# The normalised memory of a cross-attention trunk moved from SBUF to DRAM, with nine weight buffers in place of eight

## The chip, the cores and the metric

The kernel runs on one core of a Trainium2 chip. The metric is the device time of one execution in microseconds (us). The kernel before takes 1259.96 us, the median of three runs (1259.71 to 1259.99). One further execution was profiled; every trace reading below comes from that one.

## The reference

A trunk of two layers works on 256 tokens of width 1024 in float32. Each layer is half a SwiGLU feed-forward, a token mixer, a cross-attention into 256 memory tokens, and another half feed-forward. The mixer is a differential attention in layer 0 and a Mamba-2 SSD in layer 1.

```python
for i in range(DEPTH):                        # 2 layers
    h = h + 0.5 * swiglu(rmsnorm(h, ffn1_norm[i]), ffn1_w_gate[i], ffn1_w_up[i], ffn1_w_down[i])
    hn = rmsnorm(h, mix_norm[i])
    h = h + (diff_attention if i == 0 else ssd_mixer)(hn, ...)
    h = h + memory_cross_attention(rmsnorm(h, xa_norm[i]), mem, xa_mem_norm[i], xa_w_q[i], xa_w_kv[i], xa_w_o[i])
    h = h + 0.5 * swiglu(rmsnorm(h, ffn2_norm[i]), ffn2_w_gate[i], ffn2_w_up[i], ffn2_w_down[i])
return rmsnorm(h, final_norm)
```

The part that the change handles is the memory. `memory_cross_attention` computes `m = rmsnorm(mem, mem_norm)` and from it keys and values, `m @ w_kv`. The RMS factor of `mem` is the same in both layers; only the gain `xa_mem_norm[i]` differs.

## The kernel before, in words

**Weights.** All weights are streamed from HBM once, in tiles `w` of 128 partitions x 2048 float32 (1 MB, 8 KB of each partition). Their pool `wp` has eight buffers. `W.load` (L161) and `Pair.load` (L176) issue the loads on SyncE (SP); a load waits on SP until the buffer that it takes was read for the last time, and the loads behind it on SP wait with it. Every weight is used in two parts, so that float32 accuracy comes out of the fast float32r matmul: a "granule" of 1024 columns is cast on ScalarE (ACT) to `whi` (L224), and VectorE (DVE) forms the rest `wlo` (L225). Both have four buffers, and granules are cut two ahead of their use (`AHEAD`). TensorE (PE) then runs `mm3` (L262 to L264): hi x hi, lo x hi and hi x lo.

**Feed-forward.** A hidden width of 2816 is done in columns c = 0 to 4 of 512 and a half one. The first feed-forward does c = 2, 3 and 4 with a scheme of seven products in place of eight (`seven`, tile name `seven`), the three later ones c = 1 to 4. For it, sums of weight tiles are formed before they are cut. Two of the four sums of each c are DVE additions of whole tiles (`Sum.load`, L203, 128 x 2048 elements); the two others are accumulating DMAs that GpSimd (POOL) issues (L199). DVE works in order: a sum whose tile has not landed holds up every `wlo` behind it. Between the products of `seven`, granules of the down projection and of other columns (tile names `out`, `gate`, `up`) are woven in.

**Memory.** `mem_stage` loads the memory tokens in four tiles `mnat` (L685) during the first feed-forward, and `mem_prep` (L688) scales them by their RMS factor. `turn` (L701) then transposes them, two 128 x 128 transposes on PE into a PSUM tile `tin` and one ACT copy (L705), eight times, into eight tiles `memt[j]` of 128 x 256 in the `const` pool; they stay there (8 KB of each partition) to the end. Two users read them. `MemKV.prep` multiplies them by the layer's gain and splits them, `mh` on ACT (L457) and `ml` on DVE (L459), for the key and value projections. `MemKV.mix` (L1071) multiplies them once more into four tiles `my` of the pool of 28 general buffers ("slots", 128 x 512), and `combine` makes from these the sums which `seven` needs for the value projection.

**Where these run.** Hooks in the program call them. Layer 0: `prep` after the first value columns (L1006), `mix` at step (0, 4) of the mixer's out projection (`out_b`, L1043). Layer 1: `prep` first in the first feed-forward, by the key 12 (L1607), which `extras(6)` calls in the middle of column 4; `prep` again and then `mix` in the out projection of the SSD mixer at steps (1, 4) and (0, 8) (L1519). The steps of `out_b` run in the order (0, k), (1, k) for each block k.

**Order.** Only the very start is ordered by hand on every engine, and the SSD stretch on PE. Elsewhere the framework's scheduler orders each engine's instructions, so a change in one place can move instructions elsewhere.

Of the kernel before, what the change touches and what calls it, by code (L numbers as in the profile page):

```python
# [7 lines left out]
F32 = mybir.dt.float32  # L8
F32R = mybir.dt.float32r
BF16 = mybir.dt.bfloat16  # L10
I32 = mybir.dt.int32
AF = mybir.ActivationFunctionType
# [3 lines left out]
P = 128  # L16
S = 256
D = 1024
KT = D // P
# [38 lines left out]
def trunk(ctx, tc, a, out):  # L58
    nc = tc.nc


    const = ctx.enter_context(tc.tile_pool(name="const", bufs=1))
    wp = ctx.enter_context(tc.tile_pool(name="wp", bufs=8))
    hp = ctx.enter_context(tc.tile_pool(name="hp", bufs=4))
    xp = ctx.enter_context(tc.tile_pool(name="xp", bufs=8))
    sp = ctx.enter_context(tc.tile_pool(name="sp", bufs=28))
# [3 lines left out]
    dram = ctx.enter_context(tc.tile_pool(name="dram", bufs=1, space=bass.MemoryType.DRAM))  # L70

    def slot(name, dt=F32):
        return sp.tile([P, 512], dt, name=name, tag="s")

    def acc(name):
        return pacc.tile([P, 512], F32, name=name, tag="acc")

    def small_ps(name):
        return pacc.tile([P, 512], F32, name=name, tag="acc")

    def work(name, n=512, dt=F32):

        return wk.tile([P, n], dt, name=name, tag="v", bufs=6) if n <= 256 else wk.tile([P, n], dt, name=name, tag="w")


    ident = const.tile([P, P], F32, name="ident")
# [53 lines left out]
    pipe = Pipe()  # L140
# [96 lines left out]
    def use(gr):  # L237

        for g in gr:
            ready(g.at + AHEAD + 1)  # L240
            yield g
# [19 lines left out]
    def mm3(o, lh, ll, rh, rl, start, stop, onto=False):  # L261
        nc.tensor.matmul(o, lhsT=lh, rhs=rh, start=start, stop=False, skip_group_check=onto)  # L262
        nc.tensor.matmul(o, lhsT=lh, rhs=rl, start=False, stop=False, skip_group_check=onto)  # L263
        nc.tensor.matmul(o, lhsT=ll, rhs=rh, start=False, stop=stop, skip_group_check=onto)  # L264
# [161 lines left out]
    def out_b(src, nkt, lhs, fin, order, hooks={}):  # L426


        banks = [[], []]
        first, last = order[0], order[-1] + 3  # L430

        def run(*gr, half):
            if not banks[half]:
                banks[half] += [acc("out") for _ in range(2)]
            for g in use(gr):
                for k in range(g.nk):
                    kt = g.k0 + k
                    for t in range(2):
                        xh, xl = pipe.need(lhs, kt)
                        ts = slice(t * P, (t + 1) * P)  # L440
                        mm3(banks[half][t], xh[:, ts], xl[:, ts], g.hi[:, k, :], g.lo[:, k, :], kt == first, kt == last)
                        pipe.pe(0.68)
                    if kt == last:
                        fin(half, banks[half])
        for half, k0 in [(c, k) for k in order for c in range(2)]:
            if (half, k0) in hooks:
                units.append(([], hooks[half, k0]))
            w = W(src, k0, 4, half * 512, 512)
            for k in range(k0, k0 + 4, 2):
                units.append(([Gran(k, 2, (w, 0, 512))], lambda *gr, half=half: run(*gr, half=half)))  # L450

    def split_act(dst_hi, dst_lo, src, scale):

        if not isinstance(src, (list, tuple)):
            dst_hi, dst_lo, src, scale = [dst_hi], [dst_lo], [src], [scale]
        for h_, s_, c_ in zip(dst_hi, src, scale):
            nc.scalar.activation(h_, s_, AF.Copy, scale=c_)  # L457
        for h_, l_, s_, c_ in zip(dst_hi, dst_lo, src, scale):
            nc.vector.scalar_tensor_tensor(l_, s_, c_, h_.bitcast(F32), op0=ALU.mult, op1=ALU.subtract)  # L459
# [34 lines left out]
    class Norm:  # L494
# [68 lines left out]
        def turn(self, c):  # L563
            for i in range(2):
                ps = self.flip(c, i)
                self.put(4 * c + 2 * i, ps[:, 0, :], ps[:, 1, :])
# [9 lines left out]
    def v2(t, j=2):  # L576
        return t.rearrange("p (j t) -> p j t", j=j)

    def upd(scale, norm):
        def fin(c, ps):  # L580
            for t in range(2):
                if scale == 1.0:
                    nc.vector.tensor_tensor(h[t][c], ps[t], h[t][c], op=ALU.add)
                else:
                    nc.vector.scalar_tensor_tensor(h[t][c], ps[t], scale, h[t][c], op0=ALU.mult, op1=ALU.add)
            norm.add(c)
        return fin
# [57 lines left out]
    lqk2 = lqk  # L645
    lqk = lqk.rearrange("p (k d) -> p k d", k=4)
    subln = cols0[:, KT:KT + 1]
    memt = [const.tile([P, S], F32, name=f"mem{j}") for j in range(KT)]
    mcol = const.tile([P, 16], F32, name="mcol")
    mnat = [[None, None], [None, None]]  # L650
    cols1 = const.tile([P, P], F32, name="cols1")
# [7 lines left out]
    def gains(nm, l=0):  # L659
        o = rowpos[nm] + l * KT  # L660
        return cols1[:, o:o + KT]
# [26 lines left out]
    def mem_prep():  # L688
        mss = sm.tile([P, 16], F32, name="mss", tag="mss", bufs=1)
        for t in range(2):  # L690
            for c in range(2):
                junk = work("junkm", 512)
                nc.scalar.activation(junk, mnat[t][c], AF.Square, accum_out=mss[:, 2 * c + t:2 * c + t + 1])
        nc.vector.tensor_tensor(mss[:, 4:6], mss[:, 0:2], mss[:, 2:4], op=ALU.add)
        nc.vector.tensor_scalar(mcol[:, 2:4], mss[:, 4:6], 1.0 / D, EPS, op0=ALU.mult, op1=ALU.add)
        nc.gpsimd.tensor_tensor(mcol[:, 0:2], mcol[:, 2:4], neghalf[:, 0:2], op=ALU.pow)
        for t in range(2):
            for c in range(2):
                nc.scalar.activation(mnat[t][c], mnat[t][c], AF.Copy, scale=mcol[:, t:t + 1])

        def turn(j):  # L701
            ps = small_ps("tin")
            for t in range(2):
                nc.tensor.transpose(ps[:, t * P:(t + 1) * P], mnat[t][j // 4][:, (j % 4) * P:(j % 4 + 1) * P], ident)
            nc.scalar.copy(memt[j], ps[:, :S])  # L705
        for j in range(KT):
            pipe.after(6.0 + 1.0 * j, lambda j=j: turn(j))


    def mem_stage():  # L710
# [184 lines left out]
    def diff_attention(norm, nxt, kv):  # L895
# [4 lines left out]
        ot = [None] * 8  # L900
# [42 lines left out]

        def proj_fin(key):
            def fin(ps):
                if not tab:
                    def late():
                        tables()
                        rope(ps, key)
                    pipe.after(T["gate"], late)  # L950
                    return
                rope(ps, key)
            return fin
# [86 lines left out]
        for c in range(2):  # L1040
            wide([(w_in, 2048 + c * 512, 512)], norm, "v", v_fin(2 * c))
        kv.k_units(kv.k_split, cs=(0,))
        out_b(a["da_w_out"][0], KT, ot, upd(1.0, nxt), (0, 4), {(0, 4): kv.mix})  # L1043


    def split2(src, name):
# [7 lines left out]
    class MemKV:  # L1054


        def __init__(self, l):
# [4 lines left out]
            self.x = []  # L1062
            self.s = [None] * 4

        def mix(self):
            y = [slot("my") for _ in range(KT // 2)]

            def full(p):
                for j in range(2):
                    k = 2 * p + j  # L1070
                    nc.scalar.activation(v2(y[p])[:, j, :], memt[k], AF.Copy, scale=self.g[:, k:k + 1])  # L1071
            for p in range(KT // 2):
                pipe.after(1.4 * p, lambda p=p: full(p))
            combine(y, self.s, [7.0 + 1.6 * i for i in range(8)])
# [3 lines left out]

        def prep(self):
            self.x.clear()  # L1080
            for j in range(KT):
                if j % 2 == 0:
                    mh, ml = slot("mh", F32R), slot("ml", F32R)
                xh, xl = (m[:, j % 2 * S:(j % 2 + 1) * S] for m in (mh, ml))
                split_act(xh, xl, memt[j], self.g[:, j:j + 1])
                self.x.append((xh, xl))

        def k_units(self, then=None, cs=(0, 2)):
            def fin(c):
# [105 lines left out]
    def ssd(norm, nxt, kv):  # L1195
# [13 lines left out]
        yt = [None] * 16  # L1209
# [293 lines left out]
        for i in range(4):  # L1503
# [3 lines left out]
            def xs(j):  # L1507
                proj("a", w_in, 2048 + 512 * i + 256 * j, 256, norm, "xs", [fx[j]])
# [7 lines left out]
                     lambda ps, fz=fz: [f([p[:, j * 256:(j + 1) * 256] for p in ps]) for j, f in enumerate(fz)])  # L1516
            if i < 3:
                xs(1)
        out_b(a["ssd_w_out"][0], 16, yt, upd(1.0, nxt), (0, 4, 8, 12), {(1, 4): kv.prep, (0, 8): kv.mix})  # L1519
        written.append(len(units))  # L1520


# [80 lines left out]
    kvs = [MemKV(0), MemKV(1)]  # L1603
    for l in range(2):
        nx = Norm(gains("mix_norm", l), first=l == 1)
        ffn("ffn1", l, nrm, nx,
            {1: param_cols, 8: rope_tables, 9: lam_col, 12: mem_stage} if l == 0 else {12: kvs[1].prep})  # L1607
        nx2 = Norm(gains("xa_norm", l))
        kv = kvs[l]
        (diff_attention if l == 0 else ssd)(nx, nx2, kv)  # L1610
        nx3 = Norm(gains("ffn2_norm", l), mixes=True)
        cross_attention(l, nx2, kv, nx3)
        if l == 0:
            nrm = Norm(gains("ffn1_norm", 1), mixes=True)
            ffn("ffn2", l, nx3, nrm)
# [58 lines left out]
```

## Time and profile before

| what | value |
|---|---|
| median of three runs | 1259.96 us (1259.71 to 1259.99) |
| the profiled execution: its time | 1260.52 us |
| its span (first to last instruction) | 1258.7 us |
| granted TensorE clock | 0.998 |
| PE busy | 1247.5 us (99%) |
| DVE busy | 1058.3 us (84%) |
| ACT busy | 873.9 us (69%) |
| POOL busy | 161.4 us (13%) |
| moved by DMA | 269.79 MB, mean 214 GB/s |

Engines are named PE, PEld (its weight loads), DVE, ACT, POOL and SP; a "q" behind one is its instruction queue (waits and DMA issues). "L203" is line 203 of the kernel before. A row of a timeline has its start, the time from the first instruction's start to the last one's end, and behind "x" how many like instructions it joins; a bracket tells how long the engine stood idle ahead of it and what ended that.

### The profile page before, as it was taken

To read this page: it belongs to the slowest core of one execution; us is meant where nothing else is said; L and a number is where in the kernel's file an instruction comes from. 1 tells how busy PE (TensorE), PEld (TensorE's weight loads), DVE (VectorE), ACT (ScalarE), POOL (GpSimd) and SP (SyncE) were. 2 spreads that over 40 slices of the span, in tenths; PEclk is the share of its full clock that TensorE was granted. 3 is DMA by queue.
4 is the path that set the end of the run, shared out by engine and by line. 5 is a ranking of instruction groups with operands and counts; after the bars stand their busy time and mean duration, and the time that the engine had idled before them with its cause. 6 is when DMAs were issued, how large, how long until landed. Compare 5 with 4: busy or idle time off the path is not lost.

```text
span 1258.7 us, 18177 instructions
## 1 busy us (share of the span) xinstructions
PE 1247.5 (99%) x6751; PEld 1072.1 (85%) x6751; DVE 1058.3 (84%) x1451; ACT 873.9 (69%) x1392; POOL 161.4 (13%) x139
## 2 busy tenths in 40 slices
PE   9999999999999999999999999999999999999997
PEld 7887888788998888888888889999998898888886
DVE  6997887886787899888998976798899887898886
ACT  6676765586676776767776856777776766877773
POOL 1101102101100111001111000022222200011100
PEclk9999999999999999999999999999999999999999
DMA  9898965335786598986689976665643786488971
GB/s 335 261 256 236 330 236 169 133 138 159 205 236 167 157 255 272 284 268 197 178 251 277 293 245 205 201 199 168 194 142 134 179 244 185 163 228 235 291 233 34
DMA packets 158315, 269.79 MB, mean 214 GB/s; under 512 B 6889, under 2 KB 43410, under 8 KB 158226
## 3 DMA queue, kind: packets, MB, share of 16 engines
q1 hardware_dynamic: 137744, 229.75, 53.6%
q0 software_dynamic: 19744, 38.28, 17.6%
q8 instruction: 53, 0.87, 0.3%
q10 hardware_dynamic: 738, 0.59, 0.2%
q14 instruction: 36, 0.29, 0.1%
HBM read 267.52 MB, written 1.08 MB: 213 GB/s over the span
## 4 chain that ended last, share of the span: by engine, by line
PE 96%; DVE 1%; DMA 1%; issue 1%; ACT 0%; POOLq 0%; POOL 0%; SPq 0%; DVEq 0%; ACTq 0%
PE out L262 9%; PE out L264 9%; PE out L263 9%; PE seven L263 8%; PE seven L264 8%; PE seven L262 8%; PE xs L264 2%; PE xs L262 2%; PE xs L263 2%; PE htp L851 1%; PE up L264 1%; PE up L262 1%; PE up L263 1%; PE mk L262 1%; PE xq L263 1%; PE mk L264 1%
## 5 line engine op out<-in xcount | busy, mean ns | idle before, releaser
L225 DVE TENSOR_TENSOR wlo<-w,whi 128x1024 fp32r<-128x1024 f32 (+2 forms) x532 | 640.0, 1220 | 132.7 <-ACT whi L224 126.0
L224 ACT CAST whi<-w 128x1024 fp32r<-128x1024 f32 (+2 forms) x534 | 551.6, 1040 | 249.8 <-PE out L264 91.2
L262 PE MATMUL out<-whi,hid_hi 128*128 128x512 f32 x336 | 132.7, 395 | 0.0
L264 PE MATMUL out<-whi,hid_lo 128*128 128x512 f32 x336 | 131.0, 390 | 0.0
L263 PE MATMUL out<-wlo,hid_hi 128*128 128x512 f32 x336 | 130.9, 390 | 0.0
L263 PE MATMUL seven<-wlo,s_hi 128*128 128x512 f32 x272 | 106.0, 390 | 0.6 <-DVE wlo L225 0.6
L262 PE MATMUL seven<-whi,s_hi 128*128 128x512 f32 x272 | 106.1, 390 | 0.0
L264 PE MATMUL seven<-whi,s_lo 128*128 128x512 f32 x272 | 105.9, 389 | 0.0
L203 DVE TENSOR_TENSOR w<-w 128x2048 f32<-128x2048 f32 x32 | 73.2, 2287 | 5.7 <-DMA w<-in_ffn_w_gate_dram 5.3
L264 PEld LDWEIGHTS out<-whi,hid_lo 128*128 128x128 f32 x336 | 63.1, 188 | 13.4
L263 PEld LDWEIGHTS out<-wlo,hid_hi 128*128 128x128 f32 x336 | 63.2, 188 | 12.6 <-DVE wlo L225 0.2
L262 PEld LDWEIGHTS out<-whi,hid_hi 128*128 128x128 f32 x336 | 63.1, 188 | 12.4
L263 PE MATMUL seven<-wlo,xh 128*128 128x512 f32 x180 | 70.2, 390 | 1.9 <-DVE wlo L225 1.9
L199 POOL DMA_DIRECT2D w<-in_ffn_w_up_dram x30 | 36.7, 1268 | 274.4 <-DVE wlo L225 267.7
L262 PE MATMUL seven<-whi,xh 128*128 128x512 f32 x180 | 70.5, 392 | 0.0
L264 PE MATMUL seven<-whi,xl 128*128 128x512 f32 x180 | 70.1, 390 | 0.0
L199 POOL DMA_DIRECT2D w<-in_ffn_w_gate_dram x30 | 36.9, 1467 | 257.9 <-DVE w L203 114.4
L263 PEld LDWEIGHTS seven<-wlo,s_hi 128*128 128x128 f32 x272 | 51.1, 188 | 11.4 <-DVE wlo L225 1.0
L264 PEld LDWEIGHTS seven<-whi,s_lo 128*128 128x128 f32 x272 | 51.0, 188 | 10.7
L262 PEld LDWEIGHTS seven<-whi,s_hi 128*128 128x128 f32 x272 | 51.1, 188 | 10.5
L263 PEld LDWEIGHTS seven<-wlo,xh 128*128 128x128 f32 x180 | 33.8, 188 | 9.1 <-DVE wlo L225 2.3
L264 PEld LDWEIGHTS seven<-whi,xl 128*128 128x128 f32 x180 | 33.8, 188 | 7.1
(395 smaller groups left out, 3016.5 us busy)
## 6 DMA issues: line engine op xcount, KB each, us to landing
w<-in_ffn_w_up_dram SPq DMA_DIRECT2D x40, 1024.0 KB, 9.5
w<-in_ffn_w_down_dram SPq DMA_DIRECT2D x40, 1024.0 KB, 9.8
w<-in_ffn_w_gate_dram SPq DMA_DIRECT2D x38, 1024.0 KB, 6.7
w<-in_ssd_w_in_dram SPq DMA_DIRECT2D x24, 1024.0 KB, 5.5
w<-in_xa_w_kv_dram SPq DMA_DIRECT2D x16, 1024.0 KB, 5.3
w<-in_ffn_w_gate_dram POOLq DMA_DIRECT2D x30, 512.0 KB, 9.2
w<-in_ffn_w_up_dram POOLq DMA_DIRECT2D x30, 512.0 KB, 7.7
w<-in_da_w_in_dram SPq DMA_DIRECT2D x12, 1024.0 KB, 5.2
```

What stands on the lines that cost most here:

```text
L199: nc.gpsimd.dma_start(self.t[:, k:k + 2, :], w.src[r0:r0 + 2 * P, w.c0:w.c0 + w.n] .rearrange("(k p) c -> p k c", p=P), accum_op=ALU.add)
L203: nc.vector.tensor_tensor(self.t, self.l.t, w.t, op=ALU.add)
L224: nc.scalar.copy(hv, src)
L225: self.eng.tensor_tensor(self.lo[:, :, o:o + n], src, hv.bitcast(F32), op=ALU.subtract)
L262: nc.tensor.matmul(o, lhsT=lh, rhs=rh, start=start, stop=False, skip_group_check=onto)
L263: nc.tensor.matmul(o, lhsT=lh, rhs=rl, start=False, stop=False, skip_group_check=onto)
L264: nc.tensor.matmul(o, lhsT=ll, rhs=rh, start=False, stop=stop, skip_group_check=onto)
L851: nc.tensor.transpose(tp[:, j, t * P:(t + 1) * P], us[t][:, (i + j) * P:(i + j + 1) * P], ident)
```

## The change

The transposed memory `memt` becomes one DRAM tile of 128 x 2048 (1 MB). `turn` now does four transposes into one PSUM tile, one ACT copy of 128 x 512 to a slot `mt`, and one DMA write of 256 KB issued by ACT; it runs four times rather than eight. A new `fetch` takes four slots `my` and issues four 256 KB DMA reads, on ACT too. `prep` and `mix` read these slots; `mix` scales them in place. `fetch` is called four times, 16 reads in all:

- layer 0, ahead of `prep`: at the end of the second key columns (`proj_fin`, key ("k", 1));
- layer 0, ahead of `mix`: at step (0, 0) of the out projection;
- layer 1, ahead of the first `prep`: at key 12 of the first feed-forward; `prep` moves from key 12 to key 8, which is called at the end of column 4;
- layer 1, in the SSD out projection: at step (1, 4); `prep` moves from (1, 4) to (0, 8), `mix` from (0, 8) to (1, 8).

The 8 KB of each partition that this leaves free in `const` go to `wp`, which has nine buffers.

```diff
-    wp = ctx.enter_context(tc.tile_pool(name="wp", bufs=8))
+    wp = ctx.enter_context(tc.tile_pool(name="wp", bufs=9))
...
-    memt = [const.tile([P, S], F32, name=f"mem{j}") for j in range(KT)]
+    memt = dram.tile([P, KT * S], F32, name="memt")
...
-        def turn(j):
-            ps = small_ps("tin")
-            for t in range(2):
-                nc.tensor.transpose(ps[:, t * P:(t + 1) * P], mnat[t][j // 4][:, (j % 4) * P:(j % 4 + 1) * P], ident)
-            nc.scalar.copy(memt[j], ps[:, :S])
-        for j in range(KT):
-            pipe.after(6.0 + 1.0 * j, lambda j=j: turn(j))
+        def turn(i):
+            ps = v2(small_ps("tin"))
+            for j in (2 * i, 2 * i + 1):
+                for t in range(2):
+                    nc.tensor.transpose(ps[:, j % 2, t * P:(t + 1) * P], mnat[t][j // 4][:, (j % 4) * P:(j % 4 + 1) * P],
+                                        ident)
+            mt = slot("mt")
+            nc.scalar.copy(v2(mt), ps)
+            nc.scalar.dma_start(memt[:, 512 * i:512 * i + 512], mt)
+        for i in range(KT // 2):
+            pipe.after(6.0 + 2.0 * i, lambda i=i: turn(i))
...
+                if key == ("k", 1):
+                    kv.fetch()
...
-        out_b(a["da_w_out"][0], KT, ot, upd(1.0, nxt), (0, 4), {(0, 4): kv.mix})
+        out_b(a["da_w_out"][0], KT, ot, upd(1.0, nxt), (0, 4), {(0, 0): kv.fetch, (0, 4): kv.mix})
...
+        def fetch(self):
+            self.y = [slot("my") for _ in range(KT // 2)]
+            for p in range(KT // 2):
+                nc.scalar.dma_start(self.y[p], memt[:, 512 * p:512 * p + 512])
+
         def mix(self):
-            y = [slot("my") for _ in range(KT // 2)]
+            y = self.y
...
-                    nc.scalar.activation(v2(y[p])[:, j, :], memt[k], AF.Copy, scale=self.g[:, k:k + 1])
+                    nc.scalar.activation(v2(y[p])[:, j, :], v2(y[p])[:, j, :], AF.Copy, scale=self.g[:, k:k + 1])
...
-        out_b(a["ssd_w_out"][0], 16, yt, upd(1.0, nxt), (0, 4, 8, 12), {(1, 4): kv.prep, (0, 8): kv.mix})
+        out_b(a["ssd_w_out"][0], 16, yt, upd(1.0, nxt), (0, 4, 8, 12), {(1, 4): kv.fetch, (0, 8): kv.prep, (1, 8): kv.mix})
...
-            {1: param_cols, 8: rope_tables, 9: lam_col, 12: mem_stage} if l == 0 else {12: kvs[1].prep})
+            {1: param_cols, 8: rope_tables, 9: lam_col, 12: mem_stage} if l == 0 else {12: kvs[1].fetch, 8: kvs[1].prep})
```

Two places of the new order matter for the prediction. The first is DVE in layer 1's first feed-forward, where columns 2 and 3 meet. Before, it stands there (`hid_lo` is the rest of the hidden activations, `gs` the gate, `p` a product of `seven`; L203 is the sum of two weight tiles that opens column 3):

```order
L225 TENSOR_TENSOR wlo<-w,whi 128x1024 x4
L804 SCALAR_TENSOR_TENSOR gs<-gateup,rcol,gs 128x256 x2
L225 TENSOR_TENSOR wlo<-w,whi 128x1024 x3
L855 TENSOR_TENSOR hid_lo<-htp,hid_hi 128x512
L225 TENSOR_TENSOR wlo<-w,whi 128x1024 x2
L827 TENSOR_TENSOR p_6224<-seven,p_6224 128x512
L225 TENSOR_TENSOR wlo<-w,whi 128x1024
L203 TENSOR_TENSOR w<-w 128x2048
```

The same stretch of DVE with the change (its line numbers are up to 13 higher from L701 on):

```order
L225 TENSOR_TENSOR wlo<-w,whi 128x1024 x4
L808 SCALAR_TENSOR_TENSOR gs<-gateup,rcol,gs 128x256 x2
L225 TENSOR_TENSOR wlo<-w,whi 128x1024 x2
L203 TENSOR_TENSOR w<-w 128x2048
L859 TENSOR_TENSOR hid_lo<-htp,hid_hi 128x512
L225 TENSOR_TENSOR wlo<-w,whi 128x1024 x3
L831 TENSOR_TENSOR p_6229<-seven,p_6229 128x512
L225 TENSOR_TENSOR wlo<-w,whi 128x1024 x3
```

The sum has moved six instructions ahead: four `wlo`, one `hid_lo` and one product that stood before it now stand behind it. In the first feed-forward of layer 0 the sums keep their places.

The second place is ACT in the SSD out projection, at step (1, 4). Before (`mh` is the memory's high part, made straight from `mem`; `y` and `state` are the mixer's):

```order
L224 CAST whi<-w 128x1024
L1446 COPY state<-pst 128x256
L457 ACTIVATE mh<-mem_102,cols_111 128x256
L457 ACTIVATE mh<-mem_103,cols_111 128x256
L457 ACTIVATE mh<-mem_104,cols_111 128x256
L457 ACTIVATE mh<-mem_105,cols_111 128x256
L224 CAST whi<-w 128x1024
L457 ACTIVATE mh<-mem_106,cols_111 128x256
```

ACT at the same place with the change:

```order
L1459 COPY state<-pst 128x256
L1074 DMA my<-memt 128x512 x4
L224 CAST whi<-w 128x1024
L457 ACTIVATE mh<-my,cols_104 128x256
L1482 ACTIVATE junk,yss<-y 128x256 x2
L224 CAST whi<-w 128x1024
L457 ACTIVATE mh<-my,cols_104 128x256 x3
L1486 ACTIVATE y<-y,yrc 128x256 x2
```

Four reads are issued where the first `mh` stood; one cast now stands between the last read's issue and the first `mh`, which needs the first read landed.

More of the change, by code (lines that the diff above doesn't have):

```diff
@@ L1080, in prep @@
             self.x.clear()
[L1081 to L1086, printed above, removed]
+            y = self.y
+            for p in range(KT // 2):
+                mh, ml = slot("mh", F32R), slot("ml", F32R)
+                for j in range(2):
+                    k = 2 * p + j
+                    xh, xl = v2(mh)[:, j, :], v2(ml)[:, j, :]
+                    split_act(xh, xl, v2(y[p])[:, j, :], self.g[:, k:k + 1])
+                    self.x.append((xh, xl))
         def k_units(self, then=None, cs=(0, 2)):
```

## The prediction

> **What bounds the kernel now.** The page first: how busy PE is, and what the chain that ended last is made of.
>
> ```profile
> PE 1247.5 (99%) x6751; PEld 1072.1 (85%) x6751; DVE 1058.3 (84%) x1451; ACT 873.9 (69%) x1392; POOL 161.4 (13%) x139
> PE 96%; DVE 1%; DMA 1%; issue 1%; ACT 0%; POOLq 0%; POOL 0%; SPq 0%; DVEq 0%; ACTq 0%
> ```
>
> PE is busy 1247.5 of 1258.7 us, and the change leaves every matmul as it is. So at most 11.2 us are in play, and most of those lie at the ends of the program. The windows tell which do not: of all stretches of 25 us past the start only these two, besides one of 0.23 us at 775 to 800, have PE under 25.00 (columns: window, length, then busy time of PE, PEld, DVE, ACT, POOL, then granted clock, DMA share, GB/s).
>
> ```profile
> 50.00:75.00 25.00, 24.39 (x108) 19.89 (x107) 21.11 (x19) 18.96 (x23) 4.47 (x4) 1.00 1.00 261
> 100.00:125.00 25.00, 23.10 (x102) 18.61 (x101) 17.57 (x16) 14.81 (x16) 2.45 (x2) 1.00 0.87 243
> 775.00:800.00 25.00, 24.77 (x205) 24.36 (x204) 14.58 (x33) 15.99 (x29) 0.00 (x0) 1.00 0.73 230
> ```
>
> PE idles 0.61 + 1.90 + 0.23 = 2.7 us in the body of the program. The PE waits name the first two, and the PE timeline their places.
>
> ```profile
> PE seven L263 <- DVE wlo L225: 2.5, 2, 1.9
> ...
> 57.02 0.39 PE L264 MATMUL gate<-whi,xl 128*128 128x512 f32 x1
> 57.25 0.39 PE L262 MATMUL seven<-whi,s_hi 128*128 128x512 f32 x1
> 58.24 0.50 PE L263 MATMUL seven<-wlo,s_hi 128*128 128x512 f32 x1 [0.61 <-DVE wlo L225]
> ...
> 117.07 0.39 PE L262 MATMUL seven<-whi,xh 128*128 128x512 f32 x1
> 119.36 0.50 PE L263 MATMUL seven<-wlo,xh 128*128 128x512 f32 x1 [1.90 <-DVE wlo L225]
> 119.70 0.40 PE L264 MATMUL seven<-whi,xl 128*128 128x512 f32 x1
> ```
>
> Matmuls start 0.23 us apart where nothing waits (57.02 to 57.25). Start to start, the wait at 117 (call it A) costs 119.36 - 117.07 - 0.23 = 2.06 us, and its first matmul after another 0.34 - 0.23 = 0.11: 2.17 us. The wait at 57 (B) costs 58.24 - 57.25 - 0.23 = 0.76, with the same refill some 0.87 us. These two are the whole prize; both say "DVE", so the question is what held DVE.
>
> For A, DVE's timeline and the one DMA step of the chain:
>
> ```profile
> 110.58 1.21 DVE L225 TENSOR_TENSOR wlo<-w,whi 128x1024 fp32r<-128x1024 f32 x1
> 115.87 2.29 DVE L203 TENSOR_TENSOR w<-w 128x2048 f32<-128x2048 f32 x1 [4.08 <-DMA w<-in_ffn_w_gate_dram]
> 118.08 2.35 DVE L225 TENSOR_TENSOR wlo<-w,whi 128x1024 fp32r<-128x1024 f32 x2
> ...
> 106.49 9.26 DMA w<-in_ffn_w_gate_dram
> ```
>
> DVE is free at 111.79 and stands 4.08 us until the gate tile has landed at 115.75, 9.26 us after its issue. The sum, then one `wlo`, then PE: 119.36 - 115.87 = 3.49 us from sum to PE. For B:
>
> ```profile
> 49.99 3.60 DVE L225 TENSOR_TENSOR wlo<-w,whi 128x1024 fp32r<-128x1024 f32 x3 [0.57 <-ACT whi L224]
> 53.51 2.28 DVE L203 TENSOR_TENSOR w<-w 128x2048 f32<-128x2048 f32 x1
> 56.96 1.23 DVE L225 TENSOR_TENSOR wlo<-w,whi 128x1024 fp32r<-128x1024 f32 x1 [1.17 <-ACT whi L224]
> ```
>
> No load is in it: DVE works without a gap from 49.99 to 55.79, the cast waits for the sum, the `wlo` for the cast.
>
> **The change part by part.** *The ninth buffer.* A load is issued when the last reader of its buffer is done; with one buffer more, each is issued at the release that admitted its predecessor. SP's issues before A:
>
> ```profile
> 83.81 0.37 SPq L161 DMA_DIRECT2D w<-in_ffn_w_up_dram  x1
> 95.01 0.37 SPq L161 DMA_DIRECT2D w<-in_ffn_w_down_dram  x1
> ...
> 104.65 0.37 SPq L161 DMA_DIRECT2D w<-in_ffn_w_down_dram  x1
> 106.49 5.70 SPq L161 DMA_DIRECT2D w<-in_ffn_w_gate_dram  x2
> ```
>
> The gate load of A thus moves from 106.49 to 104.65, the down load of 95.01 to 83.81. What the queues do meanwhile:
>
> ```profile
> 92.00:96.00 4.00, 4.00 (x20) 3.29 (x19) 4.00 (x6) 2.75 (x5) 0.00 (x0) 1.00 0.00 1
> 96.00:100.00 4.00, 4.00 (x19) 3.34 (x18) 2.99 (x4) 2.10 (x3) 2.46 (x2) 1.00 0.97 277
> 108.00:116.00 8.00, 8.00 (x37) 6.63 (x36) 3.79 (x5) 6.19 (x7) 0.00 (x0) 1.00 1.05 389
> ```
>
> They move nothing from 92 to 96 and are full from 96 to 116. The down tile of 1 MB goes into that hole, which takes 1 MB / 389 GB/s = 2.7 us off the backlog. The gate load then lands between 104.65 + 9.26 = 113.9 (the same flight time) and 115.75 - 1.84 - 2.7 = 111.2 (issue and backlog both earlier); I take the middle, 112.5. For A to vanish, the sum must start by 115.87 - 2.06 = 113.8, so the load must land by 113.7. Gain 2.17 us, with 0 to 0.3 left over; I take 0.1. Lost altogether (0) if the backlog, not the issue, sets the landing and nothing moves.
>
> B stays: the order of DVE there is the old one, and no load waits. The 0.2 us at 775 to 800 is of another kind and stays.
>
> *Fewer, longer turns.* PE goes to the memory's transposes four times rather than eight. Each excursion has its toll in the matmul behind it:
>
> ```profile
> 180.53 0.48 PE L262 MATMUL out<-whi,hid_hi 128*128 128x512 f32 x1
> 180.84 0.39 PE L263 MATMUL out<-wlo,hid_hi 128*128 128x512 f32 x1
> 181.08 0.40 PE L264 MATMUL out<-whi,hid_lo 128*128 128x512 f32 x1
> ```
>
> 0.31 us instead of 0.23, so 0.08 each; four fewer make -0.3 us. It is on the path, since PE is busy there. The transposes themselves stay sixteen.
>
> *ACT's DMAs.* 4 writes and 16 reads are issued on ACT, which issues nothing of the kind in the body now. Price, from the two pairs at the end:
>
> ```profile
> 1251.38 0.86 ACTq L1570 DMA_DIRECT2D out_dram<-h  x2
> ```
>
> 0.43 us each, 8.6 us of ACT in all, at most 1.7 us in one go. ACT is 69% busy, and casts run two granules ahead (5.4 us of PE for two granules of 12 matmuls), so a burst of 1.7 us hides: 0. Its worst place is the SSD out projection, where the first `mh` stands one cast behind the reads and holds every later cast until its tile has landed:
>
> ```profile
> 961.50 1.71 ACT L457 ACTIVATE mh<-mem,cols 128x256 fp32r<-128x256 f32 x4
> 965.53 1.06 ACT L224 CAST whi<-w 128x1024 fp32r<-128x1024 f32 x1 [2.33 <-PE out L264]
> ```
>
> The cast after it had 2.33 us to spare even so. Against that stands a landing for which no such 256 KB read exists before; its ends are its bytes alone (0.26 MB / 389 GB/s = 0.7 us) and A's 9.26 us. At 5 us, ACT would wait 1 to 2 us within the slack; 0, up to +2 at the far end. The other three fetches stand five granules or more ahead of their use: 0. I put +0.2 here for all.
>
> A fetch carries 1 MB, 2.7 us of the queues. Two places bound whom it meets:
>
> ```profile
> 700.00:706.00 6.00, 6.00 (x31) 5.01 (x31) 5.88 (x6) 4.14 (x6) 0.00 (x0) 1.00 1.05 388
> 935.00:985.00 50.00, 50.00 (x252) 42.01 (x251) 46.12 (x72) 34.47 (x70) 14.38 (x11) 1.00 0.49 150
> ```
>
> In the SSD projection half of the queues' time is free. In layer 1's feed-forward (about 705) they are full, so a weight load there lands up to 2.7 us later. [...] I price it at 0, since the same loads start a step earlier.
>
> *Moved sums.* In the three later feed-forwards the scheduler, seeing a buffer more, puts the opening sum (L203) of columns 2, 3 and 4 ten, six and three instructions ahead. Column 3 of layer 1's first one is the tightest:
>
> ```profile
> 638.99 0.37 SPq L161 DMA_DIRECT2D w<-in_ffn_w_down_dram  x1
> 646.01 0.37 SPq L161 DMA_DIRECT2D w<-in_ffn_w_gate_dram  x1
> ...
> 643.63 2.36 DVE L225 TENSOR_TENSOR wlo<-w,whi 128x1024 fp32r<-128x1024 f32 x2 [0.45 <-ACT whi L224]
> 646.47 1.22 DVE L225 TENSOR_TENSOR wlo<-w,whi 128x1024 fp32r<-128x1024 f32 x1 [0.48 <-ACT whi L224]
> ...
> 650.64 0.39 PE L262 MATMUL out<-whi,hid_hi 128*128 128x512 f32 x1
> ...
> w<-in_ffn_w_gate_dram SPq DMA_DIRECT2D x38, 1024.0 KB, 6.7
> ```
>
> The sum now starts when the `wlo` pair ends, 645.99, or when its tile has landed. Behind it stand a `hid_lo` (0.6) and the `wlo` of 646.47, which PE needs at 650.64 + 0.23 = 650.87. Sum 2.2 + 0.6 + 1.2 = 4.0, so the sum must start by 646.8. Its load is now issued at about 639.0 to 639.4; with the median flight of 6.7 us it lands at 645.7 to 646.1: just in time. With A's flight of 9.26 it lands at 648.3 to 648.7, and PE stalls 1.5 to 1.9 us. I take the median, with +0.2 for all nine sums (0 to 5).
>
> **Sum:** -2.17 + 0.1 - 0.3 + 0.2 + 0.2 = -2.0 us; I give it as -1.9, the ACT place being the least known. The profiled execution goes from 1260.52 to 1258.6; it lies 0.56 above the median, so the median goes from 1259.96 to 1258.1. A measurement of this kernel tells about 0.2% (2.5 us) from no change, so this is "the same": faster by that would need under 1257.4.
>
> **The rivals.**
>
> *1. The sums moved ahead wait for their loads* (slower). For it: the old place of the sum had 653.44 against an issue at 646.01, 7.4 us; the new place leaves 6.6 to 7.0, under A's flight. Against it: the flight's median fits. Mechanism: DVE stands at L203 with ready `wlo` behind it. It decides from 7.6 us of flight at column 3; three such columns, one in each later feed-forward, at 1.7 us make 5.1 us: -1.9 + 5.1 = +3.2, a median of 1263.2. 17%.
>
> *2. The wait A stays.* The gate load is issued earlier, but lands when the backlog lets it; only the turns' 0.3 us and the small costs are left: 1259.5 to 1260.2. For it: full queues from 96 to 116. Against it: the hole at 92. [...] 15%.
>
> *3. B shrinks as well* (faster). The loads ahead of 50 us come a step earlier, the casts and rests before B with them, and DVE reaches the sum of 53.51 early by its gap of 0.57 us. Then -1.9 - 0.6 - 0.2 (no leftovers at A) = -2.7: 1257.2. Against it: the 0.57 is a wait for a cast, not for a load. 12%.
>
> *4. Nothing moves:* the nine buffers fill and empty as eight did; 1260.0. Within case 2's range, 3%.
>
> **How the numbers follow.** My case has the remaining 53%, 1258.1 with its own range 1257.5 to 1259.3 (A's leftover 0 to 0.3, ACT 0 to 0.9). Below it case 3 reaches 1257.2; above it cases 2 and 4 lie inside 1260.2, and in three of ten ways of case 1 only one or two columns are late, which ends at 1262 at most. So the range is 1257.3 to 1262.3: it leaves out 0.12 of case 1 and some 0.07 of case 3. Faster by over 0.2% (under 1257.4): case 3 and a sliver of mine, 0.13. Slower by over 0.2% (above 1262.5): the 0.12 of case 1. The same: 0.75.
>
> **What would show it.** Right: the gate tile of A landed before 113.7; no L203 with an idle of some us at 110 to 120; the window 100 to 125 with PE at 25.00, and the window 50 to 75 still near 24.4; four groups of four `tin` transposes. Wrong: an idle "L203 <- DMA" at columns 2 to 4 of a later feed-forward, a cast behind an `mh` that waits for `my`, or PE under 25.00 in any stretch where it was full.

## The result and the profile after

The changed kernel takes 1257.89 us, the median of 15 runs (1257.56 to 1259.29); beside it the kernel before took 1259.99 us. The ratio is 0.9981 with a 95% interval of 0.9973 to 0.9989: 2.1 us faster, a change of under 0.2%, but one that the interval tells from none. The forecast was 1258.1. The profiled execution took 1258.38 us, its span 1256.6 us.

PE's busy time and ACT's DMA queue on the page after (queue, packets, MB, share of 16 engines' span):

```profile
PE 1247.1 (99%) x6751; PEld 1071.7 (85%) x6751; DVE 1057.2 (84%) x1451; ACT 873.5 (70%) x1388; POOL 162.5 (13%) x139
...
q10 hardware_dynamic: 3618, 5.84, 1.4%
```

The memory's 5 MB are seen in q10 (0.59 MB before), and no engine's busy time has moved by more than 1.1 us. What moved is PE's idle time, 11.2 us before and 9.5 after. The windows of the changed kernel, the same three as before:

```profile
50.00:75.00 25.00, 24.37 (x108) 19.88 (x107) 21.10 (x19) 18.97 (x23) 3.85 (x4) 1.00 1.00 258
100.00:125.00 25.00, 25.00 (x112) 20.70 (x111) 19.77 (x19) 16.83 (x18) 2.45 (x2) 1.00 1.00 274
775.00:800.00 25.00, 24.77 (x205) 24.36 (x205) 15.35 (x32) 15.97 (x29) 0.00 (x0) 1.00 0.63 194
```

The 1.90 us of A are gone and nothing else has changed: B is still 0.63 us of idle, the third place 0.23. SP's issues, DVE's timeline and two of PE's matmuls at A, after:

```profile
94.69 0.37 SPq L161 DMA_DIRECT2D w<-in_ffn_w_up_dram  x1
100.32 0.37 SPq L161 DMA_DIRECT2D w<-in_ffn_w_down_dram  x1
104.36 0.37 SPq L161 DMA_DIRECT2D w<-in_ffn_w_gate_dram  x1
...
110.29 1.21 DVE L225 TENSOR_TENSOR wlo<-w,whi 128x1024 fp32r<-128x1024 f32 x1
112.79 2.29 DVE L203 TENSOR_TENSOR w<-w 128x2048 f32<-128x2048 f32 x1 [1.28 <-DMA w<-in_ffn_w_gate_dram]
115.00 2.35 DVE L225 TENSOR_TENSOR wlo<-w,whi 128x1024 fp32r<-128x1024 f32 x2
...
116.78 0.39 PE L262 MATMUL seven<-whi,xh 128*128 128x512 f32 x1
...
117.23 0.39 PE L264 MATMUL seven<-whi,xl 128*128 128x512 f32 x1
```

The gate load goes out at 104.36 rather than 106.49, as its predecessor did before, and the sum starts at 112.79 rather than 115.87. DVE still waits 1.28 us for that tile, but PE does not: 1.28 us on DVE fit inside the lead, 4.08 us did not. PE's lead over the kernel before is 117.07 - 116.78 = 0.29 us ahead of A, from the start of the program, and 119.70 - 117.23 = 2.47 us behind it: A alone gave 2.18 us.

### The profile page after: what moved, and what is told of

Read it like the earlier page. It is cut to its first block, busy times and chain, and to the rows that moved or that the text cites. A ratio compares the mean times of both kernels' runs of the same rounds, so it can differ in the third digit from the quotient of the medians.

```text
span 1256.6 us, 18186 instructions
## 1 busy us (share of the span) xinstructions
PE 1247.1 (99%) x6751; PEld 1071.7 (85%) x6751; DVE 1057.2 (84%) x1451; ACT 873.5 (70%) x1388; POOL 162.5 (13%) x139
## 4 chain that ended last, share of the span: by engine, by line
PE 94%; DMA 2%; DVE 2%; ACT 2%; issue 1%; POOLq 0%; POOL 0%; SPq 0%; ACTq 0%; DVEq 0%
PE out L262 9%; PE out L264 9%; PE out L263 9%; PE seven L263 8%; PE seven L262 8%; PE seven L264 8%; PE htp L855 1%; PE up L263 1%; PE up L264 1%; PE up L262 1%; PE xs L264 1%; PE xs L262 1%; PE xq L263 1%; PE xq L264 1%; PE xs L263 1%; PE xq L262 1%
## 5 line engine op out<-in xcount | busy, mean ns | idle before, releaser
L203 DVE TENSOR_TENSOR w<-w 128x2048 f32<-128x2048 f32 x32 | 73.2, 2287 | 2.0 <-DMA w<-in_ffn_w_gate_dram 1.5
L262 PEld LDWEIGHTS seven<-whi,xh 128*128 128x128 f32 x180 | 33.8, 188 | 6.8
```

The costliest lines, as they stand in the source:

```text
L203: nc.vector.tensor_tensor(self.t, self.l.t, w.t, op=ALU.add)
```

## The experiments

Theory: the ninth buffer is the whole gain, through A. Rivals: the gain is the moved memory's; fetches or moved sums cost something that hides behind it. All times are medians; the kernel before took 1259.93 to 1260.16 us beside them.

**Eight buffers, the rest of the change kept.**

```diff
-    wp = ctx.enter_context(tc.tile_pool(name="wp", bufs=9))
+    wp = ctx.enter_context(tc.tile_pool(name="wp", bufs=8))
```

> The change with eight weight buffers: the memory in DRAM, fetches and turns as changed. Theory (the ninth buffer is the whole gain, by the wait of 2.06 us at 117 that it ends): that wait is back, PE idle again near 2 us between 100 and 125, time 1259.6 to 1260.2. Rival (the gain is the moved memory's: longer turns, less work for ACT, another order): near the changed kernel, 1257.7 to 1258.3, and no idle at 117.

1261.01 us, ratio to before 1.0010 (1.0001 to 1.0019): A is back, and the time is over that of the kernel before and over the range that the theory gave. Its window at A, and DVE there:

```profile
100.00:125.00 25.00, 23.32 (x103) 18.75 (x102) 18.07 (x16) 15.80 (x17) 2.45 (x2) 1.00 0.87 251
...
114.79 2.29 DVE L203 TENSOR_TENSOR w<-w 128x2048 f32<-128x2048 f32 x1 [3.85 <-DMA w<-in_ffn_w_gate_dram]
```

The rival "moved memory" falls: with it alone the kernel is 0.9 us slower than before (0.1 to 2.4 by the interval). The ninth buffer is worth 1261.01 - 1257.89 = 3.1 us here, more than A.

**Nine buffers with the memory in SBUF, and its control.** The room for the ninth buffer comes from 24 slots; the control has the 24 slots and eight buffers.

```diff
-    wp = ctx.enter_context(tc.tile_pool(name="wp", bufs=8))
+    wp = ctx.enter_context(tc.tile_pool(name="wp", bufs=9))
...
-    sp = ctx.enter_context(tc.tile_pool(name="sp", bufs=28))
+    sp = ctx.enter_context(tc.tile_pool(name="sp", bufs=24))
```

> The kernel before with nine weight buffers, the memory still in SBUF; the room comes from 24 general slots in place of 28. Theory: the wait at 117 is gone, 1257.5 to 1258.1, at or slightly under the changed kernel since no fetch is paid. Rival (moved memory): 1259.7 to 1260.2.

> Control for the run before: the kernel before with 24 slots and eight weight buffers. Both theories: as before, 1259.8 to 1260.3. If fewer slots cost something by themselves, it shows here (over 1260.3).

1267.11 and 1268.44 us. The control's expectation failed: four slots fewer cost 8.3 us. The PE waits of the control name the place, in the SSD stretch:

```profile
PE pcb L1399 <- DVE c L1350: 6.4, 1, 6.4
```

ACT begins to form that `c` at 931.80, where it did so at 921.62 before. That it stands there for want of a free slot fits the edit, but was not shown.

So only the pair compares: the ninth buffer is worth 1.3 us in it, less than the 1.94 us that PE gains at A. The windows at A, control first and then nine buffers:

```profile
100.00:125.00 25.00, 23.06 (x102) 18.52 (x101) 17.84 (x16) 15.57 (x17) 2.45 (x2) 1.00 0.85 247
```

```profile
100.00:125.00 25.00, 25.00 (x112) 20.67 (x112) 19.96 (x19) 16.88 (x19) 2.45 (x2) 1.00 1.01 279
```

A ends with the memory in SBUF too. The ninth buffer does it, wherever its room comes from; slots are the wrong place to take the room.

**The later places alone.** The memory in SBUF, eight buffers, `prep` and `mix` of layer 1 at the later places.

```diff
-{(1, 4): kv.prep, (0, 8): kv.mix}
+{(0, 8): kv.prep, (1, 8): kv.mix}
...
-{12: kvs[1].prep}
+{8: kvs[1].prep}
```

> The kernel before (memory in SBUF, eight buffers) with prep and mix of layer 1 at the later places of the change, and nothing else. The memory in DRAM with eight buffers was 0.9 us slower than before, with PE waiting 0.49 us at 991 for transposes behind a late DVE and 0.33 at 1181. If the later places bring that (their work on DVE now falls beside the update of the residual), this run is 1260.4 to 1261.0 and shows the wait at 991. If the fetches or writes bring it, 1259.8 to 1260.2.

1260.32 us, beside 1260.14. That lies between the two expectations, and a difference of 0.2 us is inside the noise; but PE is full (25.00) from 975 to 1000 and from 1175 to 1200, so the waits at 991 and 1181 do not come of the later places alone. What makes the run with eight buffers slower is in the transfers or their effects.

**Transfers with eight buffers, at the old places.** Each fetch a step ahead of the old places of `prep` and `mix`; in layer 1's first feed-forward that puts it at the end of column 3.

```diff
-{(1, 4): kv.fetch, (0, 8): kv.prep, (1, 8): kv.mix}
+{(0, 4): kv.fetch, (1, 4): kv.prep, (0, 8): kv.mix}
...
-{12: kvs[1].fetch, 8: kvs[1].prep}
+{6: kvs[1].fetch, 12: kvs[1].prep}
```

> The memory in DRAM with eight buffers once more, prep and mix of layer 1 back at the places they had before the change and each fetch a step ahead of them. The first such run was 0.9 us over the kernel before, and the later places alone (memory in SBUF) cost nothing. If the transfers and their issues on ACT cost, this run is 1260.6 to 1261.2 again. If only transfers and later places together cost, by the waits at 991 and 1181, this run is 1259.7 to 1260.2 without these waits. In both cases the wait at 117 is there, 1.7 to 2.1 us.

1271.71 us: neither theory, 11.5 us slower than before. One place makes most of it. First the sum of column 4 in the run with eight buffers above, then in this one, with its fetch (ACT), the load's step of the chain, the sum (DVE), and PE behind it with its window (the clock is the third figure from the end):

```profile
681.59 2.29 DVE L203 TENSOR_TENSOR w<-w 128x2048 f32<-128x2048 f32 x1
```

```profile
671.00 0.81 ACTq L1074 DMA_DIRECT2D my<-memt  x2
671.84 0.46 ACTq L1074 DMA_DIRECT2D my<-memt  x1
...
676.47 0.33 ACTq L1074 DMA_DIRECT2D my<-memt  x1
...
675.54 14.04 DMA w<-in_ffn_w_gate_dram
...
689.71 2.29 DVE L203 TENSOR_TENSOR w<-w 128x2048 f32<-128x2048 f32 x1 [6.92 <-DMA w<-in_ffn_w_gate_dram]
...
693.19 0.80 PE L263 MATMUL out<-wlo,hid_hi 128*128 128x512 f32 x1 [5.73 <-DVE wlo L225]
...
692.00:696.00 4.00, 2.81 (x7) 2.24 (x8) 4.00 (x6) 0.00 (x0) 2.47 (x2) 0.50 0.44 69
```

The gate load went out at about the same place of the program in both (674.29 and 675.54). There it was in SBUF within 7.3 us, since the sum did not wait for it; here it flew 14.04 us, DVE stood 6.92 us, and PE was busy only 19.27 of 25 us from 675 to 700. Behind that idle its granted clock was 0.50, and matmuls started 0.43 us apart in place of 0.23 until 698.5. Three reads of 256 KB just ahead of a load that is due, and a fourth 0.9 us behind it, put 6.7 us or more on it, far over the 2.7 us of their bytes. The windows from 664 to 688 have the queues full throughout (1.05 to 1.12), but moving 391 GB/s from 668 and only 236 from 684; POOL had issued two accumulating DMAs at 677.17. Whether these took the rest was not tried.

**Fetch at the place of use.** Reads, then `prep` or `mix` at once, at the old places; nine buffers.

```diff
-{(0, 0): kv.fetch, (0, 4): kv.mix}
+{(0, 4): lambda: (kv.fetch(), kv.mix())}
...
-{(1, 4): kv.fetch, (0, 8): kv.prep, (1, 8): kv.mix}
+{(1, 4): lambda: (kv.fetch(), kv.prep()), (0, 8): kv.mix}
...
-{12: kvs[1].fetch, 8: kvs[1].prep}
+{12: lambda: (kvs[1].fetch(), kvs[1].prep())}
```

(In layer 0 `prep` has its `fetch` directly ahead of it as well.)

> The change with every fetch at the place of its use: reads, then prep or mix at once, with prep and mix at the places they had before the change. Theory (the early start hides the landing of 4 to 9 us): ACT stands behind the first mh or my until it lands, and the casts behind it with it; at two granules of lead (5.4 us) each of four places costs 0 to 3 us of PE, together 2 to 6 us, 1260 to 1264. Rival (the reads are hidden anyway): 1257.7 to 1258.3.

1263.88 us, 6.0 us over the changed kernel. Nearly all of it comes at one place, `mix` of layer 0. ACT, then DVE there, then the PE wait, and last PE behind it with its window (the clock is the third figure from the end):

```profile
305.92 0.91 ACT L1081 ACTIVATE my<-my,cols 128x256 f32<-128x256 f32 x2 [2.43 <-DMA my<-memt]
308.79 0.91 ACT L1081 ACTIVATE my<-my,cols 128x256 f32<-128x256 f32 x2 [1.96 <-DMA my<-memt]
309.60 1.97 ACT L224 CAST whi<-w 128x1024 fp32r<-128x1024 f32 x2
...
310.66 1.23 DVE L225 TENSOR_TENSOR wlo<-w,whi 128x1024 fp32r<-128x1024 f32 x1 [5.92 <-ACT whi L224]
...
PE xt L535 <- DVE h L583: 3.6, 2, 3.3
...
314.82 0.63 PE L262 MATMUL out<-whi,o_hi 128*128 128x512 f32 x1
315.24 0.63 PE L263 MATMUL out<-wlo,o_hi 128*128 128x512 f32 x1
...
312.00:316.00 4.00, 3.18 (x14) 2.62 (x15) 4.00 (x9) 3.30 (x9) 0.00 (x0) 0.81 0.06 21
```

ACT waits twice for a landing and holds a ready cast; DVE's next `wlo` waits for the cast, and the update of `h`, queued behind that `wlo`, is what PE's transposes wait for. Three queues in order carry a wait of 4.4 us on ACT to PE. And PE then starts a matmul only every 0.42 us, at a granted clock of 0.81 in that window and 0.90 from 316 to 325: after A's 2.06 us the next one followed in 0.34, after 3.3 us of idle it runs at about half pace from 314.8 to 317.8. These slow matmuls add some 1.7 us to the 3.6 us of waiting, 5.3 of the 6.0. Behind the 5.73 us of idle in the run before, the slow stretch took 5.3 us (693.19 to 698.48), here 3.0; behind A's 2.06 us there was none: from 119.70 on the matmuls start 0.23 to 0.24 us apart, at a granted clock of 1.00. Why PE slowed down behind the two longer waits was not shown. The early start of the reads is worth these 6 us: without it the change is slower than before.

**Twice the fetch.** First each read issued twice into the same tile, then four more reads in each fetch into slots of their own.

```diff
-                nc.scalar.dma_start(self.y[p], memt[:, 512 * p:512 * p + 512])
+                for _ in range(2):
+                    nc.scalar.dma_start(self.y[p], memt[:, 512 * p:512 * p + 512])
```

```diff
                 nc.scalar.dma_start(self.y[p], memt[:, 512 * p:512 * p + 512])
+            for p in range(KT // 2):
+                nc.scalar.dma_start(slot("spare"), memt[:, 512 * p:512 * p + 512])
```

> The change with each of the 16 reads of a fetch issued twice: 4 MB more traffic, 16 more issues on ACT, results the same. It doubles the price of the fetches. Theory (fetches are hidden): within 0.2 us of the changed kernel, 1257.7 to 1258.1. Rival (a fetch holds casts or weight loads): each fetch of 2 MB in a burst of some 3 us on ACT delays a cast or a load beyond its lead, PE idle by 0.5 to 2 us near 705 or 960, 1258.5 to 1260.

> The change with four more reads of 256 KB in each fetch, into slots of their own that nothing reads: the traffic and ACT issues of a fetch doubled, but without the wait for an earlier landing in the same tile that the run with each read issued twice had. If that wait was what cost 7.7 us there, this run is within 0.3 us of the changed kernel, 1257.7 to 1258.2. If the traffic or the issues of a fetch cost (weight loads delayed by 2.7 us, casts behind 3.4 us of issues), it is 1258.5 to 1262, with PE idle near 705 or 960.

1265.57 and 1258.12 us. The first does not test the traffic alone: the second read of a tile waits for the first to land, and it waits on ACT's queue with the casts behind it. ACT in layer 1's first feed-forward of that run:

```profile
720.42 0.33 ACTq L1075 DMA_DIRECT2D my<-memt  x1
720.78 0.58 ACT L827 COPY p<-seven 128x512 f32<-128x512 f32 x1 [6.71 <-DMA my<-memt]
```

The second, without that wait, is 0.2 us over the changed kernel, which is inside the spread of either. Twice the traffic and twice the issues cost nothing that can be measured where the change has put them. What cost 7.7 us in the first is a DMA on ACT that had to wait, not the 0.4 us of an issue.

**Ten buffers** (24 slots).

```diff
-    wp = ctx.enter_context(tc.tile_pool(name="wp", bufs=9))
+    wp = ctx.enter_context(tc.tile_pool(name="wp", bufs=10))
...
-    sp = ctx.enter_context(tc.tile_pool(name="sp", bufs=28))
+    sp = ctx.enter_context(tc.tile_pool(name="sp", bufs=24))
```

> The change with ten weight buffers (24 slots in place of 28). Theory: with the wait at 117 gone there is nothing left for a tenth buffer, so within 0.3 us of the changed kernel, 1257.6 to 1258.2; the wait at 57 stays at 0.8 us. Rival (slower by moved sums): the sums of the later feed-forwards stand another two or three instructions further ahead here, so if landing is short, DVE waits at L203 for a load with PE idle behind it, over 1259. Third possibility: a tenth buffer also ends the wait at 57, 1257.0.

1275.11 us, 17.2 over the changed kernel. Some 8 us of that is the price of 24 slots if it is the same as in the control above (PE waits 6.6 us at the place of the control's 6.4); no run has 24 slots and nine buffers with the memory in DRAM. Of the rest, 4 us are PE's waits for `wlo`, 4.6 us against 0.6; what is left was not traced. The PE waits, and the sum of A with its load:

```profile
PE seven L263 <- DVE wlo L225: 4.6, 5, 2.1
...
101.07 9.86 DMA w<-in_ffn_w_gate_dram
...
111.05 2.29 DVE L203 TENSOR_TENSOR w<-w 128x2048 f32<-128x2048 f32 x1 [4.13 <-DMA w<-in_ffn_w_gate_dram]
```

The load goes out 5.4 us earlier than before the change and has landed by 110.93. But with a buffer more the scheduler has put the sum four instructions further ahead, and DVE waits 4.13 us for it: the same stall as A, a little earlier. PE waits for `wlo` at five places instead of one. A is the only one of them behind a sum that waits for its load. Three stand in later feed-forwards and are of B's kind, as this one (DVE, then PE):

```profile
429.47 2.28 DVE L203 TENSOR_TENSOR w<-w 128x2048 f32<-128x2048 f32 x1
432.92 3.50 DVE L225 TENSOR_TENSOR wlo<-w,whi 128x1024 fp32r<-128x1024 f32 x3 [1.17 <-ACT whi L224]
...
434.20 0.50 PE L263 MATMUL seven<-wlo,s_hi 128*128 128x512 f32 x1 [0.76 <-DVE wlo L225]
```

The sum has its tile there; the cast waits for the sum and the `wlo` for the cast. More buffers are not more lead when the consumer is moved as far as the load.

**Eight turns instead of four.** The same DRAM tile, written from slots filled in two halves.

```diff
-        for i in range(KT // 2):
-            pipe.after(6.0 + 2.0 * i, lambda i=i: turn(i))
+        for i in range(KT):
+            pipe.after(6.0 + 1.0 * i, lambda i=i: turn(i))
```

> The change with eight turns of two transposes (two halves of one slot copied apart, one write for each pair), as before the change. The prediction priced four fewer turns at 0.3 us, so by it this is 0.3 us over the changed kernel, 1258.2. What the trace after shows (PE's lead over the kernel before grows by under 0.1 us from 180 to 192) says 1257.9 to 1258.0.

1257.87 us, as the changed kernel: the turns are worth nothing that can be measured. A visit of two transposes before, and one of four after:

```profile
180.40 0.38 PE L704 MATMUL tin<-ident,mnat 128*128 128x128 f32 x2
180.53 0.48 PE L262 MATMUL out<-whi,hid_hi 128*128 128x512 f32 x1
180.84 0.39 PE L263 MATMUL out<-wlo,hid_hi 128*128 128x512 f32 x1
```

```profile
177.76 0.60 PE L705 MATMUL tin<-ident,mnat 128*128 128x128 f32 x4
178.12 0.48 PE L262 MATMUL out<-whi,hid_hi 128*128 128x512 f32 x1
178.43 0.40 PE L263 MATMUL out<-wlo,hid_hi 128*128 128x512 f32 x1
```

From the first transpose to the second matmul behind it: 0.44 us before, 0.67 after. Less the one matmul of 0.23 in it, that is 0.21 for two transposes and 0.44 for four: 0.11 for each, however they are grouped.

**B, first try: a `wlo` on GpSimd.** The `wlo` that DVE does at 45 goes to POOL, so that DVE comes to the sums earlier.

```diff
-        return [(Gran(k, 2, (ws[k // 4], 0, 512)), step) for k in (0, 2, 4, 6)]
+        return [(Gran(k, 2, (ws[k // 4], 0, 512), eng=nc.gpsimd if k == pool else None), step) for k in (0, 2, 4, 6)]
...
-stream([(wg, 512, 512)], norm, "gate", gate_fin(1))
+stream([(wg, 512, 512)], norm, "gate", gate_fin(1), 2)
```

> The change with one wlo of the first feed-forward (the one that DVE does at about 45, ahead of the first sum) formed by GpSimd, which stands idle there. Theory (the wait at 57 is DVE's own queue of work: three wlo, sum, cast, wlo without a gap): DVE runs 1.1 us ahead from 45 on, the wait at 57 of 0.79 + 0.11 us ends, 1257.0, and PE is full from 50 to 75. Rival (a load or the cast holds it, or GpSimd's 2.6 us slow DVE beside it): unchanged, 1257.8, or slower.

1259.27 us, 1.4 us over the changed kernel, and PE is busy 23.91 us from 50 to 75 rather than 24.37. (The profiled execution took 1258.31 us; it shows this 0.46 us, not the whole 1.4.) POOL and DVE there:

```profile
43.76 2.83 POOL L225 TENSOR_TENSOR wlo<-w,whi 128x1024 fp32r<-128x1024 f32 x1 [23.28 <-ACT whi L224]
...
44.26 4.48 DVE L203 TENSOR_TENSOR w<-w 128x2048 f32<-128x2048 f32 x1
```

The sum, 2.28 us elsewhere, took 4.48: it lost 2.20 us in the 2.33 us in which POOL worked beside it. The rival's second half was right: GpSimd slowed DVE beside it. Why was not shown.

**B, second try: another order of the granules.** In the first column of `seven`, two granules of other columns stand before the second summed pair, and none before the next.

```diff
-            counts = {2: [5, 1, 1, 1, 1, 1, 1],
+            counts = {2: [5, 1, 2, 0, 1, 1, 1],
```

> The change with one granule of another column moved within the first column of seven products: two before its second summed pair and none before the next. The wait at 57 (0.79 us and 0.11 after) comes of DVE working without a gap; PE now needs that sum's wlo 2.7 us later and DVE does one wlo (1.1 us) more ahead of it, 1.6 us of lead won. Theory: the wait ends, PE is full from 50 to 75, and the time is 1256.9 to 1257.2. Rival (the wait comes back at the next pair, whose other granule is gone): 1257.7 to 1258.5.

1257.31 us, ratio to before 0.9975 (0.9965 to 0.9986). The window of B, and DVE there:

```profile
50.00:75.00 25.00, 25.00 (x112) 20.72 (x111) 22.17 (x20) 19.22 (x23) 3.18 (x3) 1.00 1.03 274
...
49.00 4.75 DVE L225 TENSOR_TENSOR wlo<-w,whi 128x1024 fp32r<-128x1024 f32 x4 [0.57 <-ACT whi L224]
53.66 2.28 DVE L203 TENSOR_TENSOR w<-w 128x2048 f32<-128x2048 f32 x1
```

B is gone and no wait has come in its place, so B was indeed the order of work on DVE. By the medians this is the fastest kernel of the study, 0.6 us under the changed one and 2.8 under before; the intervals of the two ratios overlap, so the trace shows the step more surely than the time.

## Why the prediction was right

- *A goes with the ninth buffer.* Right in mechanism and size: 2.18 us at A, where 2.17 was forecast with 0.1 left over. The load went out at its predecessor's release, the sum started at 112.79 (the bound was 113.8), and with eight buffers A is back. Rival 2 (the load lands no earlier) and rival 4 fall. The backlog gave less than the forecast's bound of 2.7 us: the sum starts 112.79 - 104.36 = 8.43 us after the issue, where it was 9.38 before, so 0.95 us. The hole that the down tile was to fill is still nearly empty:

```profile
92.00:96.00 4.00, 4.00 (x19) 3.28 (x19) 4.00 (x6) 2.89 (x4) 0.00 (x0) 1.00 0.25 65
```

- *B stays.* Right: 24.39 and 24.37 us of PE from 50 to 75. Rival 3 falls.
- *Fewer turns, -0.3.* Wrong, and the one saving of the sum that did not come: the toll counted was that of the matmul behind a visit, but a visit's transposes cost 0.11 us each, grouped or not. The fault hardly shows, since the costs set against it (0.2 for ACT, 0.2 for the sums, 0.1 of A left over) did not come either; -2.0 worked out and -2.1 measured agree partly by that luck.
- *ACT's place in the SSD projection, +0.2.* Nothing came. The rows of the changed kernel show why it looks otherwise:

```profile
958.81 1.79 ACTq L1074 DMA_DIRECT2D my<-memt  x4
963.16 1.06 ACT L224 CAST whi<-w 128x1024 fp32r<-128x1024 f32 x1 [3.99 <-DMA my<-memt]
```

  The cast is put down to the DMA, but it starts 965.53 - 963.16 = 2.37 us earlier than before, and so does the PE matmul whose end released it before (965.10 against 962.67, 2.43 us): PE's lead of 2.47 us behind A is kept, so whichever released the cast, it cost nothing. The landing price of 5 us was near: median 4.0 us, 3.1 to 8.8. But the forecast had no need to place it between 0.7 and 9.26 us. It says that no 256 KB read exists before, and the DMA view of the kernel before has sixteen, from a scratch tile in DRAM (the last figure is the median landing in us):

```profile
E<-scr SPq DMA_DIRECT2D x16, 256.0 KB, 5.8
```

- *Moved sums, +0.2.* Nothing came at nine buffers. At column 3 the load went out at 636.28, and the sum starts when the `wlo` pair ahead of it is done, without a wait:

```profile
640.93 2.36 DVE L225 TENSOR_TENSOR wlo<-w,whi 128x1024 fp32r<-128x1024 f32 x2 [0.45 <-ACT whi L224]
643.33 2.29 DVE L203 TENSOR_TENSOR w<-w 128x2048 f32<-128x2048 f32 x1
```

  The tile had landed within 7.1 us of its issue, under the 7.6 from which rival 1 was to decide. With ten buffers a sum does wait for its load with PE idle behind it, but at A, not in the three later feed-forwards that rival 1 named.
- *What stays open.* With eight buffers the moved memory costs 0.9 us, which the forecast priced at about -0.1. The later places of `prep` and `mix` alone are not the cause. The trace with eight buffers has a wait of 1.36 us for a load ahead of a sum at 1178 (0.17 before) and late transposes at 991 that the kernel before does not have; that the transfers thin out the leads, and the ninth buffer gives them back, fits this and the run with early fetches, but the link was not shown. And the forecast took 0.2% as the least that a measurement tells from no change; the interval here, 0.0011 to 0.0027 under 1, tells 0.19% from it.

## What to carry to other kernels

Read a stall back to the load and ask which release admitted that load: one buffer more moves each issue to its predecessor's release, and that difference (here 1.8 us, with 0.95 us more by a shorter flight) is what the load can gain; the kernel gains at most what PE waits behind it (here 2.18 us). Then look where the scheduler puts the consumer with the new depth, since an engine in order that reaches its consumer too soon makes the stall anew (4.13 us of DVE at A with ten buffers). A transfer issued on a busy engine's queue cost nothing measurable here (1258.12 us with twice the reads, 1257.89 without) while it waited for nothing and its reader stood a step behind; where the reader stood beside it, it cost 6 us, and a fetch beside a due load made most of 11.5 us.

## What the runs showed of the hardware that was not expected

- A float32 addition on DVE of 2.28 us took 4.48 us beside a float32 subtraction of 2.83 us on GpSimd: nearly all of the overlap was lost.
- After 3.3 us of idle PE ran at about half pace (0.42 us a matmul for 0.23, granted clock 0.81 from 312 to 316 and 0.90 from 316 to 325) for 3.0 us, and after 5.73 us of idle (0.43 us a matmul, granted clock 0.50 from 692 to 696) for 5.3 us; after 2.06 us it did not (0.23 to 0.24 us a matmul, granted clock 1.00).
- A 1 MB load flew 14.04 us, with three 256 KB reads from DRAM issued on another engine in the 5 us ahead of it and a fourth 0.9 us behind, where it had flown at most 7.3 us without.
- Transposes of 128 x 128 between matmuls cost PE 0.11 us each, in visits of two or of four.
